# Row sums of squares of x: reads moved to ScalarE's queue with two tiles, Squares four units behind, row scale five units later

## The chip, the cores and the metric

The kernel runs on one core of one Trainium2 chip. The metric is the device time of one execution in microseconds (us), given as the median of the runs. One further execution was taken with the hardware profiler; all times inside the kernel come from it. The engines are called by their names or by the profile's letters: PE is TensorE (matmul; PEld its weight loads), DVE VectorE, ACT ScalarE, POOL GpSimd, SP SyncE. ACTq, SPq and POOLq are the issue of transfers by these engines.

## The reference, cut to what matters

One layer of an encoder with two attention mixers and a SwiGLU, for 512 tokens of width 2048, in float32. The change lies in its first two lines:

```python
h = rmsnorm(x, g_mix)                 # x * rsqrt(mean(x*x over the 2048 columns) + EPS) * g_mix
proj = einsum('bsd,de->bse', h, w_in) # [qA|kA|vA|qB|kB|vB], 4608 columns
...                                   # mixers A and B, W_out, SwiGLU, final rmsnorm
```

The kernel multiplies x times the gain `g_mix` by `w_in` first and applies the row scale rsqrt(mean(x*x)) to the rows of the product afterwards. So the sums of squares over the rows of x (128 rows by 2048 columns, four times) are needed only when the first products leave PSUM, not when the multiplication begins.

## The kernel before, in words

**Products in three parts.** Every float32 matmul is made of three: each operand is split in a rounded high part and the rest as a low part, and high x high, high x low and low x high are summed (`mm3`, L222 to L224). The high part of a weight tile is a copy by ScalarE (L814 in column blocks, L275 in plain chunks), the low part a subtraction by VectorE (L817, L280). The pairs live in the eight buffers `tw`, taken in turn.

**Units.** The main loop at the end of `encoder_block` walks a list of units. A unit is one weight tile of 128 x 512, with its load, its split and its matmuls. In each turn n the loop emits, in this order, the load and the preparation of x tiles for a later unit, `row_squares(n)`, `prepare(n)` (weight loads and splits for units ahead), the matmuls of unit n, and the hooks of n. Each engine runs its instructions strictly in the order in which they were emitted; there is no scheduler. The pools only add the waits.

Units 0 to 15 are the first chunk (the columns kA and vA, called kvA): each multiplies the four row blocks of x by one weight tile, 12 matmuls. Its four PSUM banks are evicted by four ScalarE copies (L463) and stored to DRAM by POOL (L454). From unit 16 on come column blocks that use a scheme of seven products for four (Strassen-Winograd): six matmuls a unit, eight units for each of the products. In the first block m1 is units 16 to 23, m2 24 to 31, m7 32 to 39, m6 40 to 47. The units of m7 and m6 need a sum or difference of two weight tiles first (VectorE, L877). When a product is finished its two banks are evicted: `begin` (ScalarE, L925) or `close` (VectorE, L930) multiplies them by the row scale. m6 goes on in the banks of m1.

**x tiles.** `load_x(k)` brings columns 128k to 128k+127 of x, transposed (128 x 512), by SyncE's queue. `x_prep(k)` makes the high and low part with the gain: for even k a ScalarE copy with scale (L309) and a VectorE operation (L325); for odd k ScalarE scales the tile in place (L316), copies it (L318, for k = 1 L315 ahead of it) and VectorE subtracts (L319). `x_add(i)` (VectorE, four operations, L332 to L335) and `x_split(i)` (ScalarE L341 to L344, VectorE L342 to L345) make the four sums of a pair of x tiles that the column blocks need, in hooks of the first 28 units.

**Rows of x.** For the sums of squares the rows are read once more, untransposed, in eight halves of 128 x 1024 (512 KB each). There is one tile, `x_row`. From n = 6 to 22, every second n, `row_squares` emits the Square of the half that was read two turns before (ScalarE, L365, with the sum as a by-product) and then the read of the next half (SyncE, L367). `make_r1` (hook 23) adds the sums (VectorE), and takes the power -0.5 (POOL, L204). The evictions of m1 are the first users of the result.

**Queues.** SyncE issues nearly all loads in the order of emission, each after the waits for its target buffer; so one load that waits holds all later ones. The weight tiles of this part lie in `stage`, whose places are used again as soon as the low part of the former tile is made. Each transfer signals on one of eight counters, in turn over all engines' hardware queues, and waits for the transfer that used that counter before.

Of the kernel before, what the change touches and what calls it, by code (L numbers as in the profile page):

```python
# [11 lines left out]
F32 = mybir.dt.float32  # L12
BF16 = mybir.dt.bfloat16
F32R = mybir.dt.float32r
AF = mybir.ActivationFunctionType
OP = mybir.AluOpType
# [3 lines left out]
P = 128  # L20
S = 512
D = 2048
HD = 128
NT = S // P
KD = D // P
# [31 lines left out]
HEAD_RATE = (2.8, 1.3)  # L57
TURN_LAG = 5
HEADS_HELD = 4
ROWS_FROM = 6  # L60
VALUE_LAG = 6
COLUMN_BLOCKS = 3
SUM_LEAD = 6
# [3 lines left out]
def f32(ap):  # L67
    return ap.bitcast(F32)
# [3 lines left out]
def encoder_block(ctx, tc, x, w_in, g_q_a, g_k_a, w_out, w_gate_up, w_down, g_final, x_t, gains, c_ident, c_mask,  # L72
                  c_axial, c_partial, out):
    nc = tc.nc
# [3 lines left out]
    sp = ctx.enter_context(tc.tile_pool(name="slots"))  # L78
# [5 lines left out]
    def nm(base):  # L84
        counter[0] += 1
        return f"{base}_{counter[0]}"
# [68 lines left out]
    def form_pair(m, pairs, j):  # L155
        t, lo = (arena[0], m) if m < EARLY else (arena[1], m - EARLY)
        return t[:, lo:lo + 2, pairs, j]
# [7 lines left out]
    HEAD_HOMES = {"q": [[(4, 0), (4, 1)], [(4, 2), (4, 3)]], "k": [[(2, 4), (2, 5)], [(4, 4), (4, 5)]],  # L165
                  "v": [[(3, 4), (3, 5)], [(2, 0), (2, 1)]]}

    x_row = sp.tile([P, D // 2], F32, tag="rowss", bufs=1, name="rows")
    x_sums = [sp.tile([P, 4, 256], F32, tag="xsums", bufs=2, name=nm("xsums")) for _ in range(2)]

    load_x(0)
# [118 lines left out]
    def hook(n, f):  # L290
        hooks.setdefault(n, []).append(f)
# [10 lines left out]
    def x_prep(k):  # L302
        i, half = divmod(k, 2)
        src, gain = xs[k], gm[:, k:k + 1]
        view = src.rearrange("p (f c) -> p f c", c=256)
        hi, lo = (form_pair(3 * half, i, j) for j in range(2))
        if half == 0:
            for n in range(2) if k == 0 else [slice(0, 2)]:
                nc.scalar.activation(hi[:, n], view[:, n], AF.Copy, scale=gain)  # L309
            if k > 0:  # L310
                x_lo(k)
            hook(k, lambda: nc.gpsimd.dma_start(ar_dram[:, i], arena[0][:, 1, i]))
            return
        if k == 1:
            nc.scalar.activation(hi, view, AF.Copy, scale=gain)  # L315
        nc.scalar.activation(src, src, AF.Copy, scale=gain)  # L316
        if k > 1:
            nc.scalar.activation(hi, view, AF.Copy)  # L318
        nc.vector.tensor_tensor(lo, view, f32(hi), op=OP.subtract)  # L319
        hook(2 * i + 3 + i // 2, lambda: x_add(i))  # L320
        hook(2 * i + 4 + i // 2, lambda: x_split(i))

    def x_lo(k):
        hi, lo = (form_pair(0, k // 2, j) for j in range(2))
        nc.vector.scalar_tensor_tensor(lo, xs[k].rearrange("p (f c) -> p f c", c=256), gm[:, k:k + 1], f32(hi),  # L325
                                       op0=OP.mult, op1=OP.subtract)

    def x_add(i):
        a_l, a_r, b_l, b_r = (xs[2 * i + n // 2][:, n % 2 * 256:(n % 2 + 1) * 256] for n in range(4))
        s3, s2, s1, s4 = (x_sums[i % 2][:, n] for n in range(4))  # L330
        gain = gm[:, 2 * i:2 * i + 1]
        nc.vector.scalar_tensor_tensor(s1, a_r, gain, b_r, op0=OP.mult, op1=OP.add)  # L332
        nc.vector.tensor_tensor(s3, a_l, a_r, op=OP.subtract)
        nc.vector.scalar_tensor_tensor(s2, a_l, gain, s1, op0=OP.mult, op1=OP.subtract)
        nc.vector.tensor_tensor(s4, b_l, s2, op=OP.add)  # L335
# [21 lines left out]
    x_ss = small(2 * NT)  # L357

    def row_squares(n):
        t, half = divmod((n - ROWS_FROM) // 2, 2)  # L360
        if (n - ROWS_FROM) % 2 or not 0 <= n - ROWS_FROM <= 4 * NT:
            return
        if n > ROWS_FROM:
            at = 2 * t + half - 1
            nc.scalar.activation(x_row, x_row, AF.Square, accum_out=x_ss[:, at:at + 1])  # L365
        if t < NT:
            nc.sync.dma_start(x_row, x[0, t * P:(t + 1) * P, half * 1024:(half + 1) * 1024])  # L367

    def col_sums(src):
        ps = bank()  # L370
# [13 lines left out]

    tabs = {}

    hook(23, make_r1)
    hook(23, lambda: more_homes("more", wp.tile([P, 4, 512], F32, tag="more", bufs=1, name="more")))

    def table_tasks():  # L390
# [66 lines left out]
    def row_scale_of(name):  # L457
        return r1["r"]
# [448 lines left out]
    def in_block(names, lo):  # L907
        first = not blocks
        box = ColBlock(w_in, 0, lo, KD // 2, REREAD, "craw0" if first else "craw",
                       chain=("m1", "m2", "m7", "m6", "m4", "m5", "m3") if first else CHAIN, apart=first)  # L910
        blocks.append(box)
        out = {}

        def rows_of(form, i, j, f, ending=True):
            box.after(form, 0, lambda: [f(form, j, 2 * i + t, t) for t in range(2)])
            if form in box.last_of_bank and ending:
                box.after(form, 0, lambda: box.done(form))

        def begin(form, j, row, t):
            if not ends:  # L920
                ends.extend(sp.tile([P, 2, 512], F32, tag="ends", bufs=3, name=nm("ends")) for _ in range(3))
            if t == 0:
                ends.append(ends.pop(0))
            out[j, row] = ends[-1][:, t]
            nc.scalar.activation(out[j, row], box.bank_of(form)[t], AF.Copy,  # L925
                                 scale=row_scale_of(names[j])[:, row:row + 1])

        def close(form, j, row, t):
            e = out[j, row]
            nc.vector.scalar_tensor_tensor(e, box.bank_of(form)[t], row_scale_of(names[j])[:, row:row + 1], e,  # L930
                                           op0=OP.mult, op1=OP.add)
            store(names[j], row, e)

        def only(form, j, row, t):
            begin(form, j, row, t)
            store(names[j], row, out[j, row], nc.scalar)
        rows_of("m1", 0, 0, begin)
        rows_of("m7", 1, 1, begin)
        rows_of("m6", 1, 0, begin)
        rows_of("m2", 0, 0, close)  # L940
        rows_of("m5", 1, 1, close, not first)
        rows_of("m4", 1, 0, close)
        if first:
            rows_of("m5", 0, 1, begin)
            rows_of("m3", 0, 1, close)
        else:
            rows_of("m3", 0, 1, only)
# [229 lines left out]
    for f in range(0, NFF, 4):  # L1177
        box = gate_up_block(f)
# [159 lines left out]
    first = 0  # L1338
    for n in DOWN_PAIRS:
        next_forms(box, first, n)  # L1340
        for cb in range(2):
            box = down_block(first, n, cb, (first + n, cb) == (NFF // 2, 1))
        first += n

    at = [0.0]
# [64 lines left out]
    for n, u in enumerate(units):  # L1410
        share["now"], share["due"] = n, 1.0
        if n < KD:
            if n + 5 < KD:
                load_x(n + 5)
            if n + 1 < KD:
                x_prep(n + 1)
        if n < KD + 8:
            row_squares(n)
        prepare(n)
        for v in units[n + 1:n + 3]:  # L1420
            if v.early is not None:
                v.early()
                v.early = None
        u.mm(u)
        if u.post is not None:
            u.post()
        for f in hooks.pop(n, ()):
            f()
        give(1.0)
# [57 lines left out]
```

## Time and profile before

| | before |
|---|---|
| median of 3 runs | 1980.52 us (1979.97 to 1981.3) |
| the profiled execution | 1981.21 us, span 1979.4 us |
| granted TensorE clock, mean | 0.996 |
| TensorE busy | 1963.2 us, 99% of the span |
| VectorE busy | 1590.4 us, 80% |
| ScalarE busy | 1126.1 us, 57% |
| moved by DMA | 399.01 MB, mean 202 GB/s |

How to read it: busy time is the union of an engine's instructions. Because matmuls overlap, a busy TensorE is not necessarily one at its full pace: its pace is read from the distance of the starts of its matmuls, and from the granted clock of a window. A row of a timeline gives the start in us, the duration, engine, line, operation, out<-in, and in brackets how long the engine was idle before it and what it waited for. A row of the waits gives who waited for whom: total us, times, longest. A row of the windows gives length, then busy us (and instructions) of PE, PEld, DVE, ACT and POOL, then clock, busy share of the DMA engines, GB/s.

### The profile page before, as it was taken

The page shows a single profiled execution, that of the slowest core. Times are in us where ns is not written, and L with a number is a line of the kernel's source. Part 1 is how long each engine was busy: PE and PEld are TensorE (multiplying, and loading weights), DVE is VectorE, ACT ScalarE, POOL GpSimd, SP SyncE. Part 2 cuts the span into 40 slices and gives each one's busy share as a digit, 9 for nine tenths or more (in the row PEclk, how much of TensorE's full clock was granted, in tenths as well). Part 3 has the DMA queues.
Part 4 walks back from the last instruction along what each step waited for, and adds up shares of the span by engine and source line. Part 5 has one row for each costly group of instructions (what it writes and reads, how often), then busy time and mean ns, then how long its engine had stood idle before and what let it go on. Part 6 is the DMA issues. An engine that isn't in the chain of part 4 may idle for free.

```text
span 1979.4 us, 27365 instructions
## 1 busy us (share of the span) xinstructions
PE 1963.2 (99%) x8903; PEld 1617.3 (82%) x8903; DVE 1590.4 (80%) x2727; ACT 1126.1 (57%) x2045; POOL 120.4 (6%) x162
## 2 busy tenths in 40 slices
PE   9999999999999999999999999999999999999998
PEld 7688888888888888888888888888888888888886
DVE  7788678878775698877878877878789988978877
ACT  7555555565455565555555555555545666666655
POOL 0000001000000000000000000000000121111121
PEclk9899999999999999999999999999999999999999
DMA  9776684244343654845837747558467798869865
GB/s 309 235 272 200 221 262 146 69 144 128 117 133 112 211 200 156 289 150 202 297 117 249 243 144 274 192 175 298 136 211 260 210 270 259 228 144 266 235 131 166
DMA packets 230928, 399.01 MB, mean 202 GB/s; under 512 B 22784, under 2 KB 69632, under 8 KB 230656
## 3 DMA queue, kind: packets, MB, share of 16 engines
q1 hardware_dynamic: 206384, 335.03, 50.3%
q0 software_dynamic: 17200, 40.38, 9.3%
q10 hardware_dynamic: 7200, 21.85, 3.4%
q8 instruction: 69, 1.13, 0.2%
q14 instruction: 75, 0.61, 0.1%
HBM read 334.52 MB, written 62.65 MB: 201 GB/s over the span
## 4 chain that ended last, share of the span: by engine, by line
PE 92%; DMA 3%; DVE 2%; ACT 1%; issue 1%; SPq 0%; ACTq 0%; DVEq 0%; POOLq 0%; POOL 0%
PE b L222 30%; PE b L223 30%; PE b L224 30%; DMA rows<-in_x_dram 1%; PE b L586 1%; PE b L1150 1%; DMA stage<-in_w_in_dram 1%; DMA early<-in_x_t_dram 1%; PE b L1074 0%; DVE w L280 0%; PE b L536 0%; DVE ra L433 0%; DVE qA L436 0%; PE b L547 0%; DVE qA L442 0%
## 5 line engine op out<-in xcount | busy, mean ns | idle before, releaser
L222 PE MATMUL b<-tw,arena 128*128 128x512 f32 x2244 | 880.2, 392 | 4.0 <-ACT tw L814 3.4
L223 PE MATMUL b<-tw,arena 128*128 128x512 f32 x2244 | 875.9, 390 | 1.5 <-DVE tw L817 1.1
L224 PE MATMUL b<-tw,arena 128*128 128x512 f32 x2244 | 875.5, 390 | 0.0
L814 ACT ACTIVATE tw<-raw 128x512 fp32r<-128x512 f32 x924 | 557.5, 628 | 425.4 <-DVE raw L877 289.3
L817 DVE TENSOR_TENSOR tw<-raw,tw 128x512 fp32r<-128x512 f32 x924 | 619.6, 685 | 161.4 <-ACT tw L814 156.5
L222 PEld LDWEIGHTS b<-tw,arena 128*128 128x128 f32 x2244 | 422.4, 188 | 92.7 <-ACT tw L814 4.7
L223 PEld LDWEIGHTS b<-tw,arena 128*128 128x128 f32 x2244 | 422.4, 188 | 90.3 <-DVE tw L817 3.6
L224 PEld LDWEIGHTS b<-tw,arena 128*128 128x128 f32 x2244 | 422.2, 188 | 88.4
L877 DVE TENSOR_TENSOR raw<-raw,raw 128x512 f32<-128x512 f32 x528 | 360.1, 683 | 2.0 <-DMA raw<-in_w_gate_up_dram 2.0
L1223 POOL DMA_DIRECT2D x1d<-ev x76 | 66.4, 968 | 1143.4 <-ACT ev L1222 1126.8
L814 ACT ACTIVATE tw<-stage 128x512 fp32r<-128x512 f32 x140 | 85.4, 628 | 68.4 <-DVE stage L877 48.4
L817 DVE TENSOR_TENSOR tw<-stage,tw 128x512 fp32r<-128x512 f32 x140 | 93.7, 685 | 31.2 <-ACT tw L814 28.4
L222 PE MATMUL b<-w,arena 128*128 128x512 f32 x240 | 95.8, 399 | 0.0
L213 ACT ACTIVATE pTh<-b 128x512 fp32r<-128x512 f32 x64 | 38.2, 597 | 98.9 <-PE b L586 95.2
L224 PE MATMUL b<-w,arena 128*128 128x512 f32 x240 | 93.9, 391 | 0.0
L223 PE MATMUL b<-w,arena 128*128 128x512 f32 x240 | 93.5, 390 | 0.0
L1222 ACT ACTIVATE ev<-b,fixed 128x512 f32<-128x512 f32 x76 | 49.9, 683 | 29.6 <-PE b L224 29.3
L351 DVE TENSOR_TENSOR pair<-pair 128x256 f32<-128x256 f32 x120 | 45.5, 420 | 23.6 <-ACT pair L1077 22.6
L1125 DVE TENSOR_TENSOR s<-b,s 128x512 f32<-128x512 f32 x66 | 44.0, 686 | 24.8 <-PE b L224 24.8
L1153 ACT ACTIVATE pair<-b 128x512 f32<-128x512 f32 x44 | 26.3, 597 | 49.4 <-PE b L1150 49.0
L224 PEld LDWEIGHTS b<-w,arena 128*128 128x128 f32 x240 | 45.0, 188 | 10.0
L223 PEld LDWEIGHTS b<-w,arena 128*128 128x128 f32 x240 | 45.2, 188 | 9.1
(222 smaller groups left out, 1776.4 us busy)
## 6 DMA issues: line engine op xcount, KB each, us to landing
raw<-in_w_gate_up_dram SPq DMA_DIRECT2D x616, 256.0 KB, 5.3
raw<-in_w_down_dram SPq DMA_DIRECT2D x176, 256.0 KB, 6.3
stage<-in_w_in_dram SPq DMA_DIRECT2D x111, 256.0 KB, 5.2
forms<-pair SPq DMA_DIRECT2D x22, 896.0 KB, 5.3
x1d<-ev POOLq DMA_DIRECT2D x76, 256.0 KB, 6.7
fr<-forms ACTq DMA_DIRECT2D x35, 512.0 KB, 4.8
raw<-in_w_out_dram SPq DMA_DIRECT2D x32, 512.0 KB, 4.7
stage<-in_w_in_dram SPq DMA_DIRECT2D x90, 128.0 KB, 3.4
```

Source lines behind the costliest of these rows:

```text
L213: nc.scalar.activation(hi, src, AF.Copy)
L222: nc.tensor.matmul(dst, ah, bh, start=start, stop=False, skip_group_check=chained)
L223: nc.tensor.matmul(dst, ah, bl, start=False, stop=False, skip_group_check=chained)
L224: nc.tensor.matmul(dst, al, bh, start=False, stop=stop, skip_group_check=chained)
L351: nc.vector.tensor_tensor(out, x, y, op=op)
L814: nc.scalar.activation(self.pair[:, 0], self.src, AF.Copy)
L817: nc.vector.tensor_tensor(self.pair[:, 1], self.src, f32(self.pair[:, 0]), op=OP.subtract)
L877: nc.vector.tensor_tensor(t[dst], t[src[0]], t[src[1]], op=OP.add if form == "m6" else OP.subtract)
L1125: nc.vector.tensor_tensor(d[:, t], box.bank_of(form)[t], d[:, t], op=OP.add)
L1153: nc.scalar.activation(st["pair"][:, half * 1024:half * 1024 + 512], ps, AF.Copy)
L1222: nc.scalar.activation(e, box.bank_of(form)[t], AF.Copy, scale=r2["r"][:, row:row + 1])
L1223: nc.gpsimd.dma_start(x1_dram[2 * cb + j, row], e, accum_op=OP.add)
```

## The change

Three things are changed. The reads of rows are issued by ScalarE's queue into two tiles in turn; the list `ROWS_AT` says at which turns: a read at each of the first eight entries, the Square of a half two entries later (four units later in the first chunk, six after it). The row scale is made at hook 28 instead of 23, and the evictions of m1 in the first block come six units later. For the x tile k = 1 the scaling in place moves behind the matmuls of unit 1, and its low part is taken from the unscaled tile by VectorE.

```diff
-ROWS_FROM = 6
+ROWS_AT = (6, 8, 10, 12, 14, 16, 19, 22, 25, 28)
...
-    x_row = sp.tile([P, D // 2], F32, tag="rowss", bufs=1, name="rows")
+    x_rows = [sp.tile([P, D // 2], F32, tag="rowss", bufs=2, name=nm("rows")) for _ in range(2)]
...
         if k == 1:
             nc.scalar.activation(hi, view, AF.Copy, scale=gain)
-        nc.scalar.activation(src, src, AF.Copy, scale=gain)
-        if k > 1:
+            x_lo(k)
+            hook(1, lambda: nc.scalar.activation(src, src, AF.Copy, scale=gain))
+        else:
+            nc.scalar.activation(src, src, AF.Copy, scale=gain)
             nc.scalar.activation(hi, view, AF.Copy)
-        nc.vector.tensor_tensor(lo, view, f32(hi), op=OP.subtract)
+            nc.vector.tensor_tensor(lo, view, f32(hi), op=OP.subtract)
...
     def x_lo(k):
-        hi, lo = (form_pair(0, k // 2, j) for j in range(2))
+        hi, lo = (form_pair(3 * (k % 2), k // 2, j) for j in range(2))
...
     def row_squares(n):
-        t, half = divmod((n - ROWS_FROM) // 2, 2)
-        if (n - ROWS_FROM) % 2 or not 0 <= n - ROWS_FROM <= 4 * NT:
-            return
-        if n > ROWS_FROM:
-            at = 2 * t + half - 1
-            nc.scalar.activation(x_row, x_row, AF.Square, accum_out=x_ss[:, at:at + 1])
-        if t < NT:
-            nc.sync.dma_start(x_row, x[0, t * P:(t + 1) * P, half * 1024:(half + 1) * 1024])
+        if n in ROWS_AT[2:]:
+            i = ROWS_AT.index(n) - 2
+            nc.scalar.activation(x_rows[i % 2], x_rows[i % 2], AF.Square, accum_out=x_ss[:, i:i + 1])
+        if n in ROWS_AT[:-2]:
+            i = ROWS_AT.index(n)
+            t, lo = i // 2, i % 2 * 1024
+            nc.scalar.dma_start(x_rows[i % 2], x[0, t * P:(t + 1) * P, lo:lo + 1024])
...
-    hook(23, make_r1)
+    hook(ROWS_AT[-1], make_r1)
...
-        def rows_of(form, i, j, f, ending=True):
-            box.after(form, 0, lambda: [f(form, j, 2 * i + t, t) for t in range(2)])
+        def rows_of(form, i, j, f, ending=True, late=0):
+            box.after(form, late, lambda: [f(form, j, 2 * i + t, t) for t in range(2)])
...
-        rows_of("m1", 0, 0, begin)
+        rows_of("m1", 0, 0, begin, late=6 if first else 0)
...
-        if n < KD + 8:
+        if n <= ROWS_AT[-1]:
             row_squares(n)
```

The lines of the changed kernel lie up to two lower (Square L364, read L368, split L815, m1's eviction L926).

On SyncE, in the middle of the first chunk, before (`stage` and `early` hold weight tiles and x tiles, `rows` the half rows):

```order
L367 DMA rows<-in_x_dram 128x1024
L251 DMA stage<-in_w_in_dram 128x512
L140 DMA early<-in_x_t_dram 128x512 x2
L367 DMA rows<-in_x_dram 128x1024
L140 DMA early<-in_x_t_dram 128x512
L251 DMA stage<-in_w_in_dram 128x512 x2
L140 DMA early<-in_x_t_dram 128x512
L367 DMA rows<-in_x_dram 128x1024
L251 DMA stage<-in_w_in_dram 128x512 x4
L367 DMA rows<-in_x_dram 128x1024
L251 DMA stage<-in_w_in_dram 128x512 x3
```

All eight reads of rows are gone from there; the same place after the change:

```order
L251 DMA stage<-in_w_in_dram 128x512
L140 DMA early<-in_x_t_dram 128x512 x3
L251 DMA stage<-in_w_in_dram 128x512 x2
L140 DMA early<-in_x_t_dram 128x512
L251 DMA stage<-in_w_in_dram 128x512 x21
```

The 21 loads in a row are those that stood between the reads of rows. On ScalarE, the end of the reads of rows before, with the last Square, the splits of units 27 and 28 and m1's evictions; the brackets name the semaphores that each instruction waits for (DMAHW are the counters of transfers on the hardware queues):

```order
L341 ACTIVATE arena_84<-xsums_88,fixed 128x256 [waits DMASW7_49,DVE_49]
L341 ACTIVATE arena_85<-xsums_88 128x256 [waits DVE_49]
L344 ACTIVATE arena_85<-xsums_88 128x2x256 [waits DVE_49]
L365 ACTIVATE rows,fixed<-rows 128x1024 [waits DMAHW5_49]
L814 ACTIVATE tw_160<-stage 128x512 [waits DMAHW2_49,PE_49,Activation_49]
L814 ACTIVATE tw_160<-stage 128x512 [waits DMAHW3_49,PE_49,Activation_49]
L925 ACTIVATE ends_654<-b_76,fixed 128x512 [waits PE_49,Activation_49,Pool_49]
L925 ACTIVATE ends_654<-b_77,fixed 128x512 [waits PE_49]
```

The same after the change, from the sixth Square and the eighth read (L368) over the splits of units 27 to 29, the seventh Square, units 30 to 32, the eighth Square and units 33 and 34 to m1's first eviction:

```order
L364 ACTIVATE rows_87,fixed<-rows_87 128x1024 [waits DMAHW5_49]
L368 DMA rows_87<-in_x_dram 128x1024 [waits DMAHW7_49,Activation_49]
L815 ACTIVATE tw_161<-stage 128x512 [waits DMAHW0_49,PE_49]
L815 ACTIVATE tw_161<-stage 128x512 [waits DMAHW1_49,PE_49]
L815 ACTIVATE tw_161<-stage 128x512 [waits PE_49]
L364 ACTIVATE rows_86,fixed<-rows_86 128x1024 [waits DMAHW4_49]
L815 ACTIVATE tw_161<-stage 128x512 [waits DMAHW6_49,PE_49]
L815 ACTIVATE tw_161<-stage 128x512 [waits PE_49]
L815 ACTIVATE tw_161<-stage 128x512 [waits DVE_49,PE_49]
L364 ACTIVATE rows_87,fixed<-rows_87 128x1024 [waits DMAHW7_49]
L815 ACTIVATE tw_161<-stage 128x512 [waits DVE_49,PE_49] x2
L926 ACTIVATE ends_715<-b_76,fixed 128x512 [waits Pool_49]
```

The last Square has moved from ahead of units 27 and 28 to ahead of units 33 and 34, and a read stands on ScalarE that waits for two things: its own Square, and the transfer that used counter DMAHW7 before, which is the weight load of unit 31. (That load goes to a place of `stage` from which kvA was stored, and waits for that store.)

At ScalarE's start, before (first the high part of tile 1 with the gain, then its scaling in place, the splits of units 1 to 3, tile 2, the split of unit 4, tile 3):

```order
L315 ACTIVATE arena_85<-early,fixed 128x2x256
L316 ACTIVATE early<-early,fixed 128x512
L275 ACTIVATE tw_160<-stage 128x512 x3
L309 ACTIVATE arena_84<-early,fixed 128x2x256
L275 ACTIVATE tw_160<-stage 128x512
L316 ACTIVATE early<-early,fixed 128x512
L318 ACTIVATE arena_85<-early 128x2x256
L275 ACTIVATE tw_160<-stage 128x512
```

After:

```order
L315 ACTIVATE arena_85<-early,fixed 128x2x256
L275 ACTIVATE tw_161<-stage 128x512 x3
L309 ACTIVATE arena_84<-early,fixed 128x2x256
L275 ACTIVATE tw_161<-stage 128x512
L317 ACTIVATE early<-early,fixed 128x512
L319 ACTIVATE early<-early,fixed 128x512
L320 ACTIVATE arena_85<-early 128x2x256
L275 ACTIVATE tw_161<-stage 128x512
```

Tile 1's scaling (L317) now follows the split of unit 4 and stands right ahead of tile 3's own scaling (L319).

## The prediction

> **What bounds the kernel now.** I read the page's busy lines first, then the waits and the windows of the first 130 us (the change touches nothing later), then the timelines of TensorE, ScalarE and VectorE there, and the chain of waits last.
>
> ```profile
> PE 1963.2 (99%) x8903; PEld 1617.3 (82%) x8903; DVE 1590.4 (80%) x2727; ACT 1126.1 (57%) x2045; POOL 120.4 (6%) x162
> ```
> ```profile
> 40.00:60.00 20.00, 19.88 (x87) 15.81 (x85) 14.03 (x28) 13.47 (x28) 2.71 (x5) 1.00 0.87 290
> 60.00:80.00 20.00, 15.50 (x41) 10.59 (x42) 11.43 (x23) 11.99 (x24) 1.42 (x1) 0.74 0.74 239
> 80.00:100.00 20.00, 20.00 (x89) 16.52 (x88) 19.95 (x34) 10.55 (x17) 1.15 (x2) 1.00 0.50 161
> ```
>
> TensorE carries the time: only what it idles, or runs slowly, can be won. One stage stands out: between 60 and 80 us it starts 41 matmuls instead of 87 to 89, at a granted clock of 0.74. Its own timeline prices this:
>
> ```profile
> 49.90 0.39 PE L222 MATMUL b<-tw,arena 128*128 128x512 f32 x1
> ...
> 59.53 0.39 PE L224 MATMUL b<-tw,arena 128*128 128x512 f32 x1
> 61.24 0.50 PE L222 MATMUL b<-tw,arena 128*128 128x512 f32 x1 [1.32 <-ACT tw L814]
> ...
> 62.40 0.63 PE L224 MATMUL b<-tw,arena 128*128 128x512 f32 x1
> ...
> 72.97 0.80 PE L222 MATMUL b<-tw,arena 128*128 128x512 f32 x1 [1.75 <-ACT tw L814]
> ...
> 83.02 0.39 PE L222 MATMUL b<-tw,arena 128*128 128x512 f32 x1
> ...
> 95.26 0.39 PE L222 MATMUL b<-tw,arena 128*128 128x512 f32 x1
> ```
>
> Unit 16 starts at 49.90, unit 23 at 61.24, unit 27 at 72.97, unit 32 at 83.02, unit 41 at 95.26. The last two are 54 matmuls apart: 12.24 / 54 = 0.2267 us each, 1.36 a unit. Units 16 to 31 (96 matmuls) should take 21.76 us and take 83.02 - 49.90 = 33.12: **11.36 us are lost**, part idle, part at a slow clock (matmuls of 0.63 follow each other every 0.43). Both breaks wait for a weight split by ScalarE (tw, L814). Why is that late?
>
> ```profile
> 50.19 2.03 ACT L463 ACTIVATE stage<-b 128x512 f32<-128x512 f32 x4
> 52.32 1.06 ACT L365 ACTIVATE rows<-rows 128x1024 f32<-128x1024 f32 x1
> ...
> 53.37 1.14 ACT L814 ACTIVATE tw<-stage 128x512 fp32r<-128x512 f32 x2
> 54.41 0.49 ACT L341 ACTIVATE arena<-xsums,fixed 128x256 fp32r<-128x256 f32 x1
> ...
> 55.65 0.61 ACT L814 ACTIVATE tw<-stage 128x512 fp32r<-128x512 f32 x1
> ...
> 60.57 1.13 ACT L814 ACTIVATE tw<-stage 128x512 fp32r<-128x512 f32 x2
> ...
> 71.25 1.06 ACT L365 ACTIVATE rows<-rows 128x1024 f32<-128x1024 f32 x1 [2.84 <-DMA rows<-in_x_dram]
> ...
> 72.31 1.13 ACT L814 ACTIVATE tw<-stage 128x512 fp32r<-128x512 f32 x2
> ```
> ```profile
> ACT rows L365 <- DMA rows<-in_x_dram: 13.8, 6, 3.3
> ...
> SPq L367 <- ACT rows L365: 28.0, 7, 5.4
> ...
> DMA to landing us min/median/max: 4.1/5.5/7.5
> ```
> ```profile
> 53.49 6.00 DMA rows<-in_x_dram
> ...
> 66.17 5.06 DMA rows<-in_x_dram
> ...
> 72.40 0.53 ACT tw L814
> 72.97 0.80 PE b L222
> ```
>
> ScalarE stands in line behind the Square of a half row of x that hasn't landed (13.8 us in six waits). There is one tile for rows, so the next read is issued by SyncE only after the Square (28.0 us in seven waits, with weight loads queued behind). One round is landing (5.5) + Square (1.05: 52.32 to 53.37) + issue, near 7 us; the eighth ends at 72.3, while TensorE passes unit 27, whose split stands behind the eighth, at 49.90 + 11 x 1.36 = 64.9 if it may. The chain of waits says the same: reads of rows, back to back, up to the matmul at 72.97.
>
> **The change, part by part.**
>
> *Rows through ScalarE's queue, two tiles, Squares four units later.* In the order, the read of rows k+2 follows the Square of rows k at once, so SyncE no longer waits for anybody's Square, and a read has 8 to 11 us (six units of 1.36, or four first-chunk units of 12 x 0.2267) before its Square, against 4.1 to 7.5 to land. The 13.8 us of ScalarE's waiting go. ScalarE pays for eight issues. The nearest row is a store that it issues itself after an instruction it depends on:
>
> ```profile
> 213.10 0.69 ACT L925 ACTIVATE ends<-b,fixed 128x512 f32<-128x512 f32 x1 [2.77 <-PE b L224]
> 213.82 0.34 ACTq L454 DMA_DIRECT2D vB<-ends  x1
> 214.26 0.69 ACT L925 ACTIVATE ends<-b,fixed 128x512 f32<-128x512 f32 x1 [0.47 <-ACT ends L925]
> ```
>
> The next instruction starts 1.16 after the last where 0.6 is usual: about 0.5 each, 4 us in all, spread from 21 to 64 us, less than the waiting that goes. The bytes moved stay the same. Recovered at most: 11.36.
>
> What is late next? I walk the new order from the kvA evictions, which wait for TensorE's unit 15 and end at 50.2. Spacings: two splits 1.04, the three copies of an x_split 1.24 (54.41 to 55.65), Square 1.05, issue 0.5. Splits are then done for units 20, 21 at 52.9, for 22, 23 at 55.2, for 24 at 57.2, for 25, 26 at 59.5. TensorE, started at 49.65 (below), wants unit 20 at 55.1, 23 at 59.2, 24 at 60.5, 25 at 61.9, 26 at 63.3. ScalarE is 2 to 4 us ahead. VectorE has less room:
>
> ```profile
> 51.01 0.48 DVE L332 SCALAR_TENSOR_TENSOR xsums<-stage,fixed 128x256 f32<-128x256 f32 x1
> ...
> 52.59 0.69 DVE L817 TENSOR_TENSOR tw<-stage,tw 128x512 fp32r<-128x512 f32 x1
> ...
> 74.00 1.42 POOL L204 TENSOR_TENSOR fixed<-fixed 128x4 f32<-128x4 f32 x1 [20.49 <-DVE fixed L202]
> ```
>
> An x_add takes 1.58 there, a low part 0.6. Its line x_split(6), low part of 24, x_add(7), low part of 25, x_split(7), low part of 26 gives 25 at 62.0 to 62.5 and 26 at 63.4 to 64.6, where TensorE wants the second matmul of each at 62.1 and 63.5. **A new stall of 0 to 1.1; I take 0.5**, the middle.
>
> *Row scale five units later.* The eighth read is issued at about 63 to 64, lands at 68 to 71.6, and its Square stands before the splits of units 33 and 34; behind it come the sum on VectorE, the power on POOL (1.42) and the evictions of m1, which stand before the split of unit 35. That split ends between 73.5 and 76.5; its low part and the two closing additions of m2 (VectorE, behind the same scale) follow. TensorE wants unit 35 at 75.5, unit 36 at 76.9. **A stall of 0 to 2; I take 0.5**, since the median landing of 5.5 gives none at 35 and little at 36. In the trace VectorE is nearly full from 80 to 100 (19.95 of 20 us), so what it loses here it doesn't win back soon.
>
> *Second x tile scaled one unit later* (k = 1; gain 0.72 of ScalarE ahead of the first weight split).
>
> ```profile
> 7.09 0.72 ACT L316 ACTIVATE early<-early,fixed 128x512 f32<-128x512 f32 x1
> ...
> 11.45 0.63 ACT L275 ACTIVATE tw<-stage 128x512 fp32r<-128x512 f32 x1 [0.44 <-DMA stage<-in_w_in_dram]
> 11.99 0.71 ACT L316 ACTIVATE early<-early,fixed 128x512 f32<-128x512 f32 x1
> 12.73 0.63 ACT L318 ACTIVATE arena<-early 128x512 fp32r<-128x512 f32 x1
> ...
> 13.39 0.69 DVE L319 TENSOR_TENSOR arena<-early,arena 128x512 fp32r<-128x512 f32 x1 [0.99 <-ACT arena L318]
> ...
> 9.19 0.50 PE L223 MATMUL b<-tw,arena 128*128 128x512 f32 x1 [0.31 <-DVE tw L280]
> ...
> 14.99 0.39 PE L224 MATMUL b<-tw,arena 128*128 128x512 f32 x1
> ```
>
> Unit 1's second matmul comes 0.72 sooner, at 8.47. But the moved scaling now stands between the load-bound split at 11.45 and tile 3's own scaling, so tile 3's low part comes 0.62 later, done at 14.7; unit 3's third matmul, at 14.99 now, needs it and can come at 14.75: **0.25 of 0.72 stays** (0.72 if the load at 11.45 comes earlier; 0 if unit 1's weights land too late to gain; a loss is excluded, since 14.7 is ahead of 14.99 anyway). At 0 I cost two things: VectorE's later start by 0.6 and the m1 evictions six units later (m6 takes that bank again only at unit 40). VectorE runs on from there without a pause up to
>
> ```profile
> 41.44 0.75 DVE L325 SCALAR_TENSOR_TENSOR arena<-early,fixed,arena 128x512 fp32r<-128x512 f32 x1 [2.73 <-ACT arena L309]
> ```
>
> and TensorE doesn't wait for it in all that stretch; were there no slack, 0.6 would be lost.
>
> Sum: 11.36 + 0.25 - 0.5 - 0.5 = **10.6 us**. The profiled execution took 1981.21 (span 1979.4 and 1.8 around it), so 1970.6; the median of the runs shown, 1980.52, is 0.7 lower: **1969.9**. With nothing lost and the whole opening, 12.1: 1968.4.
>
> **Rivals.**
>
> (1) One break stays, at units 33 to 36, and takes the clock with it. The break at 72.97 cost 1.75 idle, and the five units after it took 10.05 instead of 6.80: 5.0 in all. Instead of my 0.5 that gives 1974.4. For it: the eighth landing at 7.5 puts the split of 35 one us late. Against: at the median landing that split is done 1 to 2 us before its time. In this trace the rate halved after an idle of 1.32 (61.24, then 62.40), so I price it so. By the Trainium skill ("TensorE: Matmul & The Clock Gate", section "The HAM clock gate") the half rate comes after an idle window of some 3.4 us; a break of 1 to 2 us would then cost its idle time alone, and this rival would end near 1971.5. The trace disagrees.
>
> (2) The engines' share is the limit, not the queue: two reads in flight take twice as long each, 11 instead of 5.5. Then two rows take 11 + 2 x 1.05 + 0.5, so 6.8 a row, about what a round takes now; from 21 us on the eighth Square ends near 75, three to four us after unit 33's split is due, and the Squares before it hold TensorE too: two breaks of 5.0 would leave 1979 (1977 to 1980). For it: 0.87 of the DMA engines busy from 40 to 60. Against: weight loads stand several deep beside each read already. The Trainium skill ("DMA: Bandwidth & Descriptors", section "Issuing engines are not separate DMA queues") says that issuing from several engines saves only issue time, which alone would leave the time at 1980; the wait that goes here is one on a buffer, of which it doesn't speak.
>
> (3) Slower: a row read now waits on ScalarE's queue, also for the earlier transfer whose counter it takes over. The eighth takes that of unit 31's weight load, which itself waits until a store of the kvA evictions has landed; the splits of unit 27 on stand behind it. Evictions to 50.2 and two landings of 5.5 make 61 to 62, and ScalarE comes there at 63 to 64. Slower begins where it is held until 72 (8 us, and 3.3 for the clock): two landings of 11 in a row, where the longest seen is 7.5. Then 1982 to 1985.
>
> **How the numbers follow.** The forecast (1968.4 to 1972) has 0.72, rival 1 0.17, rival 2 0.07, rival 3 0.04. The range goes from 1968.2 to 1975.0: it takes in rival 1 and leaves out 2 and 3. A measurement tells 0.2% (4 us) from no change; the forecast and rival 1 are both faster by more: faster 0.89, same 0.07, slower 0.04.
>
> **What would show it.** Right: in the windows 60 to 80 us has 80 or more matmuls at a clock of 1.00; ScalarE's waits for rows fall from 13.8 to under 3; the waits of SyncE on Squares are gone; unit 32 starts near 72.5. The terms: TensorE waits for tw near 62 to 64 (VectorE) and near 75 to 77. Wrong: a clock under 0.9 in that window, row landings of 10 us, ScalarE's queue waiting on weight loads, or new waits past 130 us, of which the order shows no cause.

## The result, and the profile after

The changed kernel takes 1972.24 us (median of 5 runs, 1972.08 to 1972.8) against 1980.52 (1979.97 to 1981.3): a ratio of 0.9958, 95% interval 0.9944 to 0.9973. Forecast was 1969.9 (1968.4 to 1972), range 1968.2 to 1975.0. So 8.3 us went where 10.6 were forecast: inside the range, and 0.24 above the forecast's own bounds. Its profiled execution took 1972.09 with a span of 1970.3, so by the profiles 9.1 us went.

The busy line and the windows of the changed kernel (length, then busy us and instructions of PE, PEld, DVE, ACT, POOL, then clock, share of the DMA engines, GB/s):

```profile
PE 1958.3 (99%) x8903; PEld 1615.1 (82%) x8903; DVE 1590.8 (81%) x2727; ACT 1126.1 (57%) x2045; POOL 120.3 (6%) x162
```
```profile
40.00:60.00 20.00, 20.00 (x90) 16.57 (x89) 15.85 (x33) 17.75 (x34) 2.71 (x5) 1.00 0.80 268
60.00:80.00 20.00, 19.40 (x85) 15.43 (x84) 18.58 (x35) 13.04 (x24) 2.58 (x3) 1.00 0.93 325
80.00:100.00 20.00, 20.00 (x90) 16.57 (x89) 19.91 (x34) 12.45 (x21) 0.00 (x0) 1.00 0.41 135
```

Between 60 and 80 us TensorE has 85 matmuls at a clock of 1.00 where it had 41 at 0.74. Its timeline there, the starts of units 16, 25 (first two matmuls), 26, 32 and 41:

```profile
49.93 0.39 PE L222 MATMUL b<-tw,arena 128*128 128x512 f32 x1
...
62.17 0.39 PE L222 MATMUL b<-tw,arena 128*128 128x512 f32 x1
62.87 0.50 PE L223 MATMUL b<-tw,arena 128*128 128x512 f32 x1 [0.31 <-DVE tw L818]
...
64.14 0.39 PE L222 MATMUL b<-tw,arena 128*128 128x512 f32 x1
64.81 0.50 PE L223 MATMUL b<-tw,arena 128*128 128x512 f32 x1 [0.28 <-DVE tw L818]
...
72.88 0.39 PE L222 MATMUL b<-tw,arena 128*128 128x512 f32 x1
...
85.11 0.39 PE L222 MATMUL b<-tw,arena 128*128 128x512 f32 x1
```

Units 16 to 31 take 72.88 - 49.93 = 22.95 us instead of 33.12; 21.76 would be without any loss. Two small stops remain: the second matmul of units 25 and 26, the one that needs the low part, starts 0.70 and 0.67 after the first instead of 0.23. The matmul behind each of them comes 0.33 or 0.34 later instead of 0.23, and the next few still a little late: a further 0.3, so 1.2 in all. The waits of the first 130 us, and the view of the tile of the rows:

```profile
PEld b L223 <- DVE tw L818: 1.4, 2, 0.7
...
PE b L223 <- DVE tw L818: 0.6, 2, 0.3
...
ACT tw L815 <- ACT rows L364: 0.4, 1, 0.4
```
```profile
L368 ACTq DMA_DIRECT2D rows<-in_x_dram x8: 334/335/352, 20.7 to 63.9; - x8
L364 ACT ACTIVATE rows<-rows x8: 1045/1046/1053, 32.7 to 69.6; 128x1024 f32<-128x1024 f32 x8
...
DMA to landing us min/median/max: 4.3/5.6/7.3
```

The row that gave 13.8 us, ScalarE waiting for rows, is gone, and so is SyncE's wait for Squares; a read lands as fast as before (median 5.6 against 5.5). Where TensorE then loses to VectorE is seen in the chain of waits:

```profile
62.13 0.68 DVE tw L818
...
63.13 0.42 DVE arena L344
63.55 0.60 DVE arena L347
64.15 0.61 DVE tw L818
64.81 0.50 PE b L223
```

### The profile page after: what moved, and what is told of

Same layout as the page of the kernel before. It is cut to its first block, busy times and chain, and to the rows that moved or that the text cites. A ratio compares the mean times of both kernels' runs of the same rounds, so it can differ in the third digit from the quotient of the medians.

```text
span 1970.3 us, 27367 instructions
## 1 busy us (share of the span) xinstructions
PE 1958.3 (99%) x8903; PEld 1615.1 (82%) x8903; DVE 1590.8 (81%) x2727; ACT 1126.1 (57%) x2045; POOL 120.3 (6%) x162
## 3 DMA queue, kind: packets, MB, share of 16 engines
q1 hardware_dynamic: 205232, 330.84, 49.9%
## 4 chain that ended last, share of the span: by engine, by line
PE 92%; DVE 4%; ACT 1%; issue 1%; DMA 1%; ACTq 0%; DVEq 0%; POOLq 0%; SPq 0%; POOL 0%
PE b L222 30%; PE b L224 30%; PE b L223 30%; PE b L587 1%; PE b L1151 1%; DVE tw L818 1%; DMA raw<-in_w_down_dram 0%; DMA fr<-forms 0%; DVE raw L878 0%; PE b L1075 0%; DVE w L280 0%; PE b L537 0%; DVE arena L1202 0%; ACT tw L815 0%; DVE ra L434 0%
## 5 line engine op out<-in xcount | busy, mean ns | idle before, releaser
L815 ACT ACTIVATE tw<-raw 128x512 fp32r<-128x512 f32 x924 | 557.2, 628 | 426.5 <-DVE raw L878 290.8
L815 ACT ACTIVATE tw<-stage 128x512 fp32r<-128x512 f32 x140 | 85.4, 628 | 69.4 <-DVE stage L878 45.0
```

The lines of the kernel that those rows point to most:

```text
L815: nc.scalar.activation(self.pair[:, 0], self.src, AF.Copy)
```

## The experiments

Two lengths tell the runs apart, taken from the starts of TensorE's matmuls in each profile: units 16 to 31, called the stage here (21.76 us without a loss), and units 32 to 40 (12.24 without a loss). What comes ahead of unit 16, the opening, differs between executions and is a matter of its own (below). Ratios are to the kernel before, run beside each series (its median there was 1980.22, 1980.57 or 1980.68), with 95% intervals.

| kernel | median us | ratio | unit 16 starts | units 16-31 | units 32-40 |
|---|---|---|---|---|---|
| before | 1980.52 | | 49.90 | 33.12 | 12.24 |
| k = 1 alone | 1980.36 | 0.9999 [0.999, 1.0008] | 50.98 | 31.75 | 12.24 |
| one tile, ScalarE's queue | 1983.64 | 1.0015 [1.0006, 1.0024] | 55.67 | 29.69 | 12.24 |
| one tile, later timetable | 1976.79 | 0.9981 [0.9973, 0.999] | 48.99 | 25.19 | 15.67 |
| second tile alone | 1973.29 | 0.9962 [0.9949, 0.9974] | 49.33 | 25.11 | 12.24 |
| changed, scale at 23 | 1972.52 | 0.9961 [0.9947, 0.9975] | 49.32 | 24.78 | 12.24 |
| changed | 1972.24 | 0.9958 [0.9944, 0.9973] | 49.93 | 22.95 | 12.24 |
| changed, once more | 1971.83 | 0.9954 [0.9942, 0.9967] | 51.08 | 22.94 | 12.24 |
| changed without k = 1 | 1972.18 | 0.9955 [0.9942, 0.9967] | 51.00 | 22.93 | 12.24 |
| changed, SyncE's queue | 1971.33 | 0.9952 [0.994, 0.9965] | 50.86 | 22.39 | 12.24 |
| changed, no rows | 1970.05 | 0.9947 [0.9935, 0.996] | 50.05 | 21.76 | 12.24 |
| changed, VectorE eased | 1969.48 | 0.9943 [0.9931, 0.9956] | 49.18 | 21.76 | 12.24 |
| SyncE's queue, eased | 1971.12 | 0.9949 [0.9935, 0.9962] | 51.05 | 21.76 | 12.24 |

**The changed kernel with the reads on SyncE's queue.**

```diff
-            nc.scalar.dma_start(x_rows[i % 2], x[0, t * P:(t + 1) * P, lo:lo + 1024])
+            nc.sync.dma_start(x_rows[i % 2], x[0, t * P:(t + 1) * P, lo:lo + 1024])
```

> The changed kernel, but the rows are read by SyncE's queue as before: two tiles and Squares four units behind, without the change of queue. My theory (the lead of a read over its Square is what counts, since ScalarE no longer stands behind a Square whose row hasn't landed): most of the 8.3 us stays; SyncE again waits for Squares, but for a read four units ahead, so 1972 to 1975, ScalarE's waits for rows under 3 us, 80 or more matmuls in 60 to 80 us. Rival (the queue counts: weight loads held behind a row read that waits for a Square make the splits late): the break between units 22 and 28 stays, with a clock under 0.9 in that window, and the time is 1978 or more.

1971.33, 0.7 below my range, although SyncE still waits for Squares for 20.2 us (28.0 in the kernel before):

```profile
SPq L368 <- ACT rows L364: 20.2, 6, 7.2
```

The queue carries none of the gain. Loads held behind these waits didn't matter: from 16 to 130 us no split of this kernel waits for a weight load. Units 16 to 31 even lose 0.56 less than in the changed kernel: only unit 26 stops there.

**The kernel before with the reads on ScalarE's queue.** One tile, timetable as before.

```diff
-            nc.sync.dma_start(x_row, x[0, t * P:(t + 1) * P, half * 1024:(half + 1) * 1024])
+            nc.scalar.dma_start(x_row, x[0, t * P:(t + 1) * P, half * 1024:(half + 1) * 1024])
```

> The kernel before, but the reads of rows are issued by ScalarE's queue: the change of queue without the second tile and without the longer lead. My theory: SyncE's 28 us of waiting on Squares go and nothing is gained by that, since a Square still follows its read by two units (2.7 us from unit 16 on) and a read takes 4.1 to 7.5 us to land; ScalarE still waits for rows 10 us or more, the break at unit 27 stays, 1978 to 1982 (no shorter round than landing + Square + issue, near 7 us). Rival (the queue): 1971 to 1974, with no break.

1983.64: slower, by 3.1 us (3.4 against the kernel before in the same series, 1980.22), and 1.6 above my upper end. The tile's view, and one of ScalarE's issues with what stands around it:

```profile
L365 ACT ACTIVATE rows<-rows x8: 1057/1060/1072, 27.8 to 74.6; 128x1024 f32<-128x1024 f32 x8
...
  DMA rows<-in_x_dram: 14.2, 7
```
```profile
63.42 1.06 ACT L365 ACTIVATE rows<-rows 128x1024 f32<-128x1024 f32 x1 [2.31 <-DMA rows<-in_x_dram]
64.39 0.19 ACT L365 ACTIVATION_READ_ACCUMULATOR rows<-rows 128x1 f32 x1
64.61 0.34 ACTq L367 DMA_DIRECT2D rows<-in_x_dram  x1
64.99 1.15 ACT L814 ACTIVATE tw<-stage 128x512 fp32r<-128x512 f32 x2 [0.41 <-ACT rows L365]
```

ScalarE waits as long as before (14.2), and each issue costs it 0.5 on top: the split starts 0.60 after the read-out of the sum does (64.39, 64.99), where without an issue between them it is 0.10 (66.11 and 66.21 in the kernel with the second tile alone, below). The eighth Square starts at 74.6 instead of 71.3. By the Trainium skill ("DMA: Bandwidth & Descriptors", section "Issuing engines are not separate DMA queues") another issuing engine saves issue time only. The trace agrees: this run gains nothing by it and pays for the issue on an engine that is in the way.

The loss itself lies in the first chunk. TensorE stops 1.27 us at unit 12 and 1.97 at unit 14, both times for an x tile that ScalarE prepares late (L309), and unit 16 starts at 55.67 instead of 49.90; units 16 to 31 then take 3.4 us less than in the kernel before. The longer stop, in TensorE's timeline:

```profile
48.17 0.50 PE L222 MATMUL b<-tw,arena 128*128 128x512 f32 x1 [1.97 <-ACT arena L309]
```

In that chunk the second and third read landed after 7.9 and 7.1 us, against 4.1 and 6.0 in the kernel before. So the issues and the later landings both hold ScalarE up there; what each of them costs, and why these reads landed later, isn't shown.

**Only k = 1.** In the kernel before:

```diff
-        nc.scalar.activation(src, src, AF.Copy, scale=gain)
+            x_lo(k)
+            hook(1, lambda: nc.scalar.activation(src, src, AF.Copy, scale=gain))
```

> The kernel before with only the x tile k = 1 changed. My theory from the changed kernel's trace: unit 1 starts no sooner because its weights' high parts wait for their loads, and unit 16 starts at 49.9 in both, so 0: 1980.0 to 1981.0, within 0.3 us of the kernel before. Rival (what the prediction took): 0.25 us less. Second rival (the part moves ScalarE and VectorE enough to matter at the break): 1 us or more in either direction.

1980.36, ratio 0.9999: nothing, within the 2 us that the interval leaves. The break is there: 45 matmuls between 60 and 80 us. A gain of 0.25 us couldn't be seen by this.

**The changed kernel without k = 1** (the same lines, undone).

> The changed kernel with the scaling of x tile k = 1 where it was before; the rows' part stays. My theory: the same as the changed kernel, 1971.9 to 1972.8, all of the gain sits between units 16 and 32. Rival (the moved scaling gives or costs something): 1972.5 to 1973.5 if the moved scaling gave 0.25 to 0.7, 1971 to 1971.8 if it cost as much. It also shows whether a read of forms that is late near 1650 us, with 1 us lost after it, comes again when the rest is the same.

1972.18 (1970.16 to 1972.4), the stage the same to 0.02 us. No pause near 1692 us in this profile.

**One tile with a later timetable,** SyncE's queue.

```diff
+    ROWS_LATE = (6, 8, 10, 12, 14, 17, 21, 25, 28)   # Square of the former half, then the next read
...
-    hook(23, make_r1)
+    hook(28, make_r1)
...
-        rows_of("m1", 0, 0, begin)
+        rows_of("m1", 0, 0, begin, late=6 if first else 0)
```

> The kernel before, one tile on SyncE's queue, but with a later timetable: reads at turns 6, 8, 10, 12, 14, 17, 21, 25, each Square at the next entry (28 the last), row scale at 28 and the evictions of m1 six units later as in the changed kernel. A read so has two first-chunk units (5.4 us) or four later units (5.4 us) before its Square instead of 2.7. Theory A (the timetable is what counts: the Square stood too soon behind its read, and the eighth stood behind unit 27): 1972 to 1976, a clock of 0.95 or more in 60 to 80 us, ScalarE's waits for rows halved. Theory B (a second tile is needed, since with one tile the read can't be issued before the former Square and the round of landing, Square and issue, near 7 us, is longer than 5.4): the break stays, 1978 or more.

1976.79, between the two ranges: 3.8 of the 8.3 us. The waits, the windows and TensorE's timeline of this kernel:

```profile
ACT rows L366 <- DMA rows<-in_x_dram: 13.3, 6, 3.2
```
```profile
60.00:80.00 20.00, 15.92 (x66) 11.75 (x65) 12.98 (x26) 11.53 (x22) 1.42 (x1) 1.00 0.97 328
```
```profile
66.07 0.50 PE L223 MATMUL b<-tw,arena 128*128 128x512 f32 x1 [1.84 <-DVE tw L818]
66.41 0.40 PE L224 MATMUL b<-tw,arena 128*128 128x512 f32 x1
66.65 0.40 PE L222 MATMUL b<-tw,arena 128*128 128x512 f32 x1
```

ScalarE still waits 13.3 us for rows, against my "halved". So theory B is right on the cause: with one tile each round holds ScalarE, and the stops only move (units 24 to 36). But the rate fell behind none of them, not even behind one of 1.84 us, so they cost little beyond their own length: 6.9 us in both stages (25.19 + 15.67 - 34.0) against 11.4 before. That neither theory had.

**The second tile alone.** The kernel before with two tiles, a Square two reads behind, all else as it was.

```diff
-    x_row = sp.tile([P, D // 2], F32, tag="rowss", bufs=1, name="rows")
+    x_rows = [sp.tile([P, D // 2], F32, tag="rowss", bufs=2, name=nm("rows")) for _ in range(2)]
+    ROWS_AT = (6, 8, 10, 12, 14, 16, 18, 20, 22, 23)   # row scale stays at 23, reads on SyncE
```

> The kernel before with one thing changed: a second tile for rows, so that a Square stands two reads behind (four turns; the last Square at 23). Reads stay on SyncE's queue at turns 6 to 20, the row scale at hook 23, the evictions of m1 and the x tile k = 1 as before. Theory A (the second tile, two reads under way at once, carries the gain; queue, later scale and k = 1 add nothing): 1971.5 to 1973.5, ScalarE's waits for rows under 4 us, 75 or more matmuls in 60 to 80 us. Theory B (ScalarE's queue or the later scale is needed with it, since SyncE still waits for Squares with weight loads behind): 1975 or more.

1973.29: theory A, 7.4 us by this edit alone. ScalarE waits 1.8 us for rows, once, and 60 to 80 us holds 75 matmuls at a clock of 1.00. What it doesn't bring is seen on ScalarE:

```profile
65.15 1.06 ACT L364 ACTIVATE rows<-rows 128x1024 f32<-128x1024 f32 x1 [1.84 <-DMA rows<-in_x_dram]
66.11 0.19 ACT L364 ACTIVATION_READ_ACCUMULATOR rows<-rows 128x1 f32 x1
66.21 0.61 ACT L815 ACTIVATE tw<-stage 128x512 fp32r<-128x512 f32 x1
67.86 1.26 ACT L926 ACTIVATE ends<-b,fixed 128x512 f32<-128x512 f32 x2 [1.04 <-POOL fixed L204]
69.01 1.66 ACT L815 ACTIVATE tw<-stage 128x512 fp32r<-128x512 f32 x3
```

The last Square waits for its row, the evictions of m1 for the scale, and the splits behind them are late: TensorE stops 0.41 at 66.87 and 0.65 at 69.69.

**The changed kernel with the scale at hook 23.**

```diff
-ROWS_AT = (6, 8, 10, 12, 14, 16, 19, 22, 25, 28)
+ROWS_AT = (6, 8, 10, 12, 14, 16, 18, 20, 22, 23)
...
-        rows_of("m1", 0, 0, begin, late=6 if first else 0)
+        rows_of("m1", 0, 0, begin, late=0 if first else 0)
```

> The changed kernel (two tiles, ScalarE's queue) with the row scale where it was: reads at 6 to 20 every second turn, Squares four turns behind but the last at 23, row scale at hook 23, the evictions of m1 not late. Theory A (the second tile and four units of lead carry the gain): the last Squares stand 4 to 5.4 us behind their reads, ScalarE waits 1 to 4 us in all for rows and runs 2 to 4 us ahead there, so 1972 to 1974. Theory B (the later timetable of rows and scale carries the gain): a break near units 25 to 28 again with a lower clock, 1976 to 1981.

1972.52, theory A. By the medians the later scale (and with it the later last Squares) can't be told from nothing; in the profiles the stage is 24.78 against 22.95, one stop more, of the same kind:

```profile
69.37 0.50 PE L222 MATMUL b<-tw,arena 128*128 128x512 f32 x1 [0.67 <-ACT tw L815]
```

**The changed kernel without reads and Squares of rows.**

```diff
-        if n in ROWS_AT[2:]:
...
+        if n == ROWS_AT[0]:
+            nc.gpsimd.memset(x_ss, 1024.0)
```

> The changed kernel without the eight reads of rows and their Squares; the sums of squares are set to a constant, so the row scale is not that of x. It bounds what the rows cost after the change. My theory: nothing in that stage waits for rows any more; what is left, 0.9 us at units 25 and 26, is VectorE's and stays: 1971 to 1972.5. Rival (the 4 MB of reads still cost by the DMA engines' share, or the eight issues and Squares make ScalarE late): 1970 or less, and no stall at units 25 and 26.

1970.05, below my range and next to the rival's, and no stop at units 25 and 26, as the rival had it. My theory was half wrong: the stop stands in VectorE's order, which is the same here, but whether it comes depends on when VectorE gets there, and that on ScalarE's Squares and issues. The start of the last x_add, in the changed kernel, with SyncE's queue, and without rows:

```profile
60.55 0.48 DVE L334 SCALAR_TENSOR_TENSOR xsums<-early,fixed 128x256 f32<-128x256 f32 x1
```
```profile
60.93 0.48 DVE L334 SCALAR_TENSOR_TENSOR xsums<-early,fixed 128x256 f32<-128x256 f32 x1
```
```profile
59.09 0.48 DVE L334 SCALAR_TENSOR_TENSOR xsums<-early,fixed 128x256 f32<-128x256 f32 x1
```

That is 10.62, 10.07 and 9.04 after unit 16 began, and the stage loses 1.19, 0.63 and 0: what VectorE comes later, TensorE loses, beyond some slack. All that the rows still cost the changed kernel there is this 1.2 us, 0.56 of it by ScalarE's queue.

**VectorE eased.** The last x_add one unit later, the last x_split two.

```diff
-        hook(2 * i + 3 + i // 2, lambda: x_add(i))
-        hook(2 * i + 4 + i // 2, lambda: x_split(i))
+        hook(2 * i + 3 + i // 2 + 1 * (i == 7), lambda: x_add(i))
+        hook(2 * i + 4 + i // 2 + 2 * (i == 7), lambda: x_split(i))
```

> The changed kernel with the last x_add one unit later and the last x_split two units later (hooks 21 and 23 instead of 20 and 21; their results are used from unit 39 on). In VectorE's row two low parts stand ahead of the x_add instead of one, and two ahead of the x_split. Theory (the stall at units 25 and 26 is VectorE's order, 1.6 us of additions ahead of a low part that is due): the second matmul of 25 and 26 waits no more, 0.9 us less: 1971.0 to 1971.7 median, and unit 32 starts 0.9 sooner against unit 16. Rival (VectorE's total work up to unit 40 is the limit, so that what is put off is missing later): the stall moves to units 28 to 40 and the time stays 1972 to 1973.

1969.48 (1969.04 to 1970.82), 1.5 below my range. The stage has no loss left: VectorE now makes two low parts in a row ahead of the additions and two behind,

```profile
59.18 1.28 DVE L818 TENSOR_TENSOR tw<-stage,tw 128x512 fp32r<-128x512 f32 x2
60.38 0.48 DVE L334 SCALAR_TENSOR_TENSOR xsums<-early,fixed 128x256 f32<-128x256 f32 x1
...
61.62 0.42 DVE L337 TENSOR_TENSOR xsums<-early,xsums 128x256 f32<-128x256 f32 x1
61.97 1.29 DVE L818 TENSOR_TENSOR tw<-stage,tw 128x512 fp32r<-128x512 f32 x2
```

and units 16 and 32 start 21.76 apart:

```profile
49.18 0.39 PE L222 MATMUL b<-tw,arena 128*128 128x512 f32 x1
...
70.94 0.39 PE L222 MATMUL b<-tw,arena 128*128 128x512 f32 x1
```

Nothing was missing later. The medians are 2.4 to 2.8 below those of the changed kernel; 1.2 us of that are shown; the rest is within what the opening varies (unit 16 starts at 49.2 here, at 49.9 and 51.1 there).

**SyncE's queue and VectorE eased** (the read on `nc.sync`, the last x_add three units later, the last x_split four).

> Two tiles with the reads on SyncE's queue (as in the run with the changed timetable and SyncE's queue) and the last x_add three units later, the last x_split four units later (hooks 23 and 25); the rest as in the changed kernel. Theory: the stall of 0.45 us at unit 26 goes, and without the eight issues ScalarE is 4 us less busy, which nobody waits for: 1968.5 to 1970.0, the same as the eased kernel with ScalarE's queue (1969.48). Rival (the queue matters once VectorE doesn't): outside that, 1970.5 or more if SyncE's waits for Squares hold weight loads, under 1968.3 if ScalarE's issues cost something.

1971.12, outside my range by 1.1 and in the rival's, but its cause isn't seen: the stage is 21.76, without a loss, as in the eased kernel with ScalarE's queue. This execution's unit 16 started at 51.05 instead of 49.18, and that is the difference between the two profiles: from there to the end of the span both take 1918.4. Whether the medians differ by the same isn't shown, since one execution of each was profiled.

**The changed kernel once more.**

> The changed kernel once more, for a second profile and five more times. If the pause of 0.62 us that TensorE makes near 1692 us (a read of forms that landed late near 1654) belongs to this kernel's phase, it comes again; if it is a matter of the single execution, it is absent or elsewhere. The opening (unit 16 at 49.9 in the first profile) may differ by up to 1.5 us, as in the other profiles, since the weight rate of the first matmuls rises at different times. Median 1971 to 1973.

1971.83 (1970.2 to 1972.63). The stage is the same to 0.01 us, the pause near 1692 is absent, the opening 1.2 us longer. So the pause belongs to the first execution. In it ScalarE waited 1.29 us for a read of forms at 1654.34, and TensorE stopped later; that the one led to the other isn't shown:

```profile
1692.38 0.50 PE L222 MATMUL b<-tw,arena 128*128 128x512 f32 x1 [0.62 <-ACT ev L1223]
```

The matmuls between 1640 and 1720 us of the kernel before took 80.95 us in that execution, 80.01 in this one and 80.01 to 80.11 in all other runs.

## Why the prediction was right, and where not

*11.36 us recoverable.* Right: 33.12 became 22.95, and 21.76 with VectorE eased or the rows left out. The cause was named rightly, ScalarE in line behind a row that hasn't landed: the second tile alone takes its waits from 13.8 to 1.8 us and 7.4 us off the time.

*SyncE's queue.* The prediction laid weight loads held behind SyncE's 28.0 us of waits beside that cause and put queue and tile in one step. The queue was no part of it: second tile alone 7.4 us of gain, queue alone a loss of 3.1, two tiles on SyncE 20.2 us of waits and the best of the stages but for the eased ones and the one without rows. In the profiles, units 16 to 40 take 45.36 before, 37.35 with the second tile, 34.63 with the later timetable (and k = 1) as well, 35.19 with ScalarE's queue on top. In these runs SyncE's loads are far enough ahead to be held.

*ScalarE's issues at 0.* Mis-sized: each is 0.5 as estimated, but the cover named, that it is less than the waiting that goes, doesn't hide them from VectorE, whose inputs come later: 0.56 us of the stage. By the medians (1971.33 against 1972.24 and 1971.83) it can't be told.

*Stop at units 25 and 26, 0.5 (0 to 1.1).* Place and mechanism as the prediction worked them out (the low part of 25 was forecast for 62.0 to 62.5 and is done at 62.13 + 0.68 = 62.8); it measured 0.9, and 0.3 more in the matmuls right behind: 1.2 in all, over twice the 0.5 and just above the 1.1.

*Scale later, a loss of 0.5 at units 35 and 36.* No stop there, and with the scale at 23 there is one at 69.4 (24.78 against 22.95), so by the profiles the term had the wrong sign; that run also moved the last Squares, and its median doesn't tell. I priced only what the scale's users lose by it, not what ScalarE gains that no longer stands behind the scale. The eighth read went out at 63.95, as forecast, and its Square found the row there.

*Opening, +0.25.* The prediction excluded a loss and took a gain; neither can be seen. Unit 16 starts between 48.99 and 51.08 (but for the kernel with one tile on ScalarE's queue), with and without the edit.

*The sum.* For the profiled execution 1970.6 was forecast and 1972.09 came. Of the 1.5 us the opening is 0.25, the stage 0.2 (10.17 gained where 11.36 - 0.5 - 0.5 = 10.36 were expected) and the pause near 1692 us, which only this execution had, 0.94. The other 0.8 of the 2.3 between forecast and median is how the profiled executions stand to their medians: 0.7 above before, 0.15 below after. That the stage came within 0.2 is luck in part: of its two losses of 0.5 one measured 1.2 and the other nothing. And the sign named for it, unit 32 near 72.5, doesn't follow from the terms, which give 49.65 + 21.76 + 0.5 = 71.9; it came at 72.88.

*The rivals.* (1) no break at 33 to 36, 12.24 us in every two-tile run. Its price rested on the break at 72.97 and on the rate falling after an idle of 1.32 us; a stop of 1.84 left the rate alone (above), so the break need not have cost 5.0. (2) The changed kernel hardly tests it: its reads are issued 4.6 to 7.6 us apart and overlap by 1.4 at most. With the second tile alone the first two overlap by 4.5 us and land after 7.8 and 8.2, against 7.5 for the first read of the kernel before and the 11 of this rival. (3) ScalarE's queue was not held at the eighth read.

## What to carry to other kernels

An in-order engine that stands behind a load's consumer pays for the landing; a second buffer, with the consumer one more read behind, takes that away, whichever queue issues the read. Ask of each wait in a queue whether the work behind it has a deadline: the 20.2 us left with two tiles on SyncE's queue cost nothing that the stage shows. When the big wait is gone, walk the next engine's order for short work that is due behind long work that isn't: one such pair moved was worth the rest of the stage.

## What the runs showed that I had not expected

The fall of TensorE's rate isn't set by the length of a stop. In the kernel with one tile and the later timetable 1.84 us left it at 0.23 a matmul; in the kernel with k = 1 alone, TensorE's timeline shows 1.09 halving it:

```profile
67.67 0.63 PE L222 MATMUL b<-tw,arena 128*128 128x512 f32 x1 [1.09 <-ACT tw L816]
68.40 0.80 PE L223 MATMUL b<-tw,arena 128*128 128x512 f32 x1
68.99 0.63 PE L224 MATMUL b<-tw,arena 128*128 128x512 f32 x1
69.42 0.63 PE L222 MATMUL b<-tw,arena 128*128 128x512 f32 x1
```

The granted clock adds that the fall lasts whole stretches of 3.41 us: it is 0.50 from 67.89 to 71.31 here, and from 62.17 to 65.58 and from 72.41 to 79.24 in the kernel before. In the stretch of that length ahead of 67.89 TensorE was busy for 1.67 us; in the kernel with one tile and the later timetable it was busy for 1.65 from 62.40 to 65.81, and the clock stayed at 1.00. So its busy time in such a stretch doesn't decide alone either, and what does wasn't settled.

The opening, too, takes different times in executions of one kernel. The first twelve matmuls of the changed kernel, in its two profiles:

```profile
4.86 3.95 PE L764 MATMUL b<-tw,arena 128*128 128x512 f32 x12 [0.44 <-DVE tw L1404]
```
```profile
5.01 5.41 PE L764 MATMUL b<-tw,arena 128*128 128x512 f32 x12 [0.59 <-DVE tw L1404]
```

5.41 / 12 = 0.45 each is about the half rate throughout; in 3.95 the rate rises on the way. Of the 1.5 us 1.2 are still there at unit 16. All 13 profiles fall in two groups by this: in five, one execution each of five kernels, unit 1 starts at 10.0 to 10.3 us and unit 16 at 50.86 to 51.08; in the other eight unit 1 starts at 7.8 to 8.7, and unit 16, but for the kernel with one tile on ScalarE's queue, at 48.99 to 50.05. By the Trainium skill ("TensorE: Matmul & The Clock Gate", section "The HAM clock gate") the rate is set by windows of some 3.4 us that run freely, so that the moment of the rise varies from run to run. These two openings agree with that. That it re-throttles after an idle window doesn't fit the halving after 1.09 us, unless a stretch with TensorE busy for 1.67 of 3.41 us counts as idle.
